# A hybrid recurrent and attention layer: heads innermost in q and k, keys stored twice, and a counted order of the recurrent projection's products

## The chip, the cores and the metric

One core of one Trainium2 chip runs the whole layer in one launch. The metric is the device time of an execution in microseconds (us). All sums below are made against one profiled execution and its trace.

## What is computed

The reference is one layer over 1024 latent tokens of width 1024 and 256 context tokens. Cut to what matters here:

```python
xn = modulate(rms_norm(x), sh1, sc1)                 # and cn for the context tokens
yg, xr, q, k, v, gr, gn = split_in(xn @ w_in + b_in) # each 1024 wide
xr = centred_dwconv(xr, conv_w, conv_b)              # 4 taps
# for both directions: r, i = sigmoid(xr @ wa), sigmoid(xr @ wi), 16 blocks of 64
a = exp(log_a); b = sqrt(-expm1(2 * log_a)) * (i * xr)
h = linear_recurrence(a, b, h0)                      # a scan over the tokens
y_rnn = (h_forward + h_backward) * gelu(yg)
q4, k4 = axial_rope(q), axial_rope(k)                # 16 heads of 64
y_na = neighbourhood_attention(q4, k4, v4, kc4, vc4, rpb)
mix = sigmoid(gr) * (y_rnn @ w_proj_rnn) + sigmoid(gn) * (y_na @ w_proj_na)
x = x + g1 * (mix @ w_out)
x = x + g2 * expert_choice_moe(modulate(rms_norm(x), sh2, sc2), ...)   # 16 experts
return rms_norm(x) * final_norm
```

## The kernel before, in words

Every product is made exact to about float32 by splitting each operand into a rounded high part and the rest: a product is three matmuls (`mm3`, lines 187 to 189): high by high, high by low, low by high. High parts are casts, low parts are subtractions. There is no scheduler: each engine runs its instructions in the order in which the program is written, and where two parts run beside each other, `weave` takes turns between two generators by a cost that each adds up in `done`.

The stages run one after the other.

1. **q, k, v** (about 60 to 389 us of the span). For each of four groups `g` of four heads, `rotary` makes 512 tokens at a time of q, then of k: TensorE (PE) fills PSUM tiles `pq`, ScalarE (ACT) evicts them to `qr`, VectorE (DVE) and GpSimd (POOL) rotate, and `out_parts` (lines 474 to 484) splits the result into `ohi` (ACT) and `olo` (DVE), three buffers each, and stores both to `d_q` or `d_k` in DRAM through SP's queue. A row of such a tile is one column of one head, and the four heads of the group are the outermost part of the row's number. v is evicted by DVE (`vo`, line 616) and stored by SP.
2. **The recurrent branch** (389 to 847 us), `stage_lru`. `proj` makes the eight blocks' inputs, gates and gelu branches; its products land in eight PSUM buffers `pp`. `chain` does, for each block `j`: the convolution `xc` (POOL, then DVE, lines 776 and 779), its high and low parts `xch` (ACT, line 783) and `xcl` (DVE), the gate matmuls, tanh evictions `tr`, `ti` (ACT), exponentials, and the scans (DVE). `tail(j)` adds both directions (POOL, line 736), multiplies by the gelu branch (DVE, line 744), splits the result into high (ACT, line 748) and low (POOL, line 749; DVE for the last block) and stores it to `d_yrh`, `d_yrl`. ACT also evicts the gates `tg` (line 729) and casts the streamed weights `w0h`, `w1h` (line 181).
3. **Attention and the recurrent projection** (847 to 1214 us), `stage_attn`. `attend` has 128 units `n` (pair of heads, strip of 128 queries, head of the pair). At step `n` it issues `score(n)` (four matmuls `sp`, then DVE's add of the bias and maximum, line 908), `turn(n-3)` (five transposes `pt` of 128 columns, copied out by ACT to `et`, line 933), `values(n-5)` (matmuls `pv`, for two units at every second step), `expo(n)` (ACT), and after the turn change `scale(n-1)` (DVE). Loads of the next heads (`load_head`, at steps 2 and 6 of 16), biases (4) and values (8) are written into the same steps, on SP's queue. `project` multiplies `w_proj_rnn` by y_rnn (from `d_yr`, tiles `x0h`, `x1h`, `x0l`, `x1l`, 1 MB each, fetched once for each half of the tokens): 128 products of three matmuls `pr`, 16 output blocks of 8 products each, two products to a turn of `weave`. Its weights come through the `Stream` S: 1 MB chunks in two raw buffers, each split as a whole by one ACT cast and one DVE subtraction of 128x2048 when a chunk is taken.
4. **Merge, router and experts** (1214 us to the end), not touched by the change.

SBUF is a stack at one end: attention's tiles take the place of the recurrent branch's, so a load into one waits until the old tile's last reader is done. Before, the first biases and v lie, among others, over `lwr0` (which serves as the last gate buffer) and `gel`.

The order inside attention is set by these lines:

```python
for n in range(N + 6):                 # attend: score(n), then
    if 0 <= n - 3 < N:
        turn(n - 3)
        done += 0.5
...
weave(attend(), project())
```

Of the kernel before, what the change touches and what calls it, by code (L numbers as in the profile page):

```python
# [55 lines left out]
IDLE = 1  # L56
A1, A2 = 3, 4
# [9 lines left out]
class Stream:  # L67
# [33 lines left out]
    def split(self, most=9, defer=False, pieces=1):  # L101
# [3 lines left out]
        while self.nsplit < min(self.nload, most) and self.chunks[self.nsplit][2] and self.pfree:  # L105
# [19 lines left out]
            self.nsplit += 1  # L125

# [47 lines left out]
class Kernel:  # L174
# [28 lines left out]
    def run(self):  # L203
# [16 lines left out]
        self.d_k = self.dram.tile([16, 128, NT], F32R, name="d_k")  # L220
# [95 lines left out]
    def stage_qkv(self):  # L316
# [337 lines left out]
    def stage_lru(self):  # L654
        nc, I, S = self.nc, self.I, self.S
        tgp, ctg = self.open_("tgp", side="right", bufs=1)
        p, cp = self.open_("lru2", side="right", bufs=1)
        last, clast = self.open_("lru3", side="right", bufs=1)
# [76 lines left out]
        def tail(j, M, done, step):  # L735
# [19 lines left out]
        def chain():  # L755
# [3 lines left out]
            for j in range(9):  # L759
# [23 lines left out]
                nc.scalar.copy(xch, xc)  # L783
# [55 lines left out]
        cfirst.__exit__(None, None, None)  # L839
        clast.__exit__(None, None, None)  # L840
        cp.__exit__(None, None, None)
# [5 lines left out]
    def stage_attn(self):  # L847
# [10 lines left out]
        def load_head(h):  # L858
# [101 lines left out]
        def attend():  # L960
            done = 0.0
# [6 lines left out]
            for n in range(N + 6):  # L968
                if n < N:
# [17 lines left out]
                    done += 0.55  # L987
                if 0 <= n - 3 < N:
                    turn(n - 3)
                    done += 0.5  # L990
                if 0 <= n - 5 < N:
                    values(n - 5)
                    done += 1.2 * (n % 2 == 0)
                if n < N:
                    expo(n)
                yield done
# [3 lines left out]
        def project():  # L1000
            done = 5.0
            yield done
            f = 1.75

# [17 lines left out]
            fetch_gate(0, 0)  # L1022
            for hf in range(2):
                cs = slice(hf * 512, (hf + 1) * 512)
                yh, yl = fetch(hf)
                done += 12.0
                yield done
                for i in range(4):
                    hi, lo = S.take8()
                    for x in range(2):  # L1030
# [5 lines left out]
                        for k in range(8):  # L1036
                            self.mm3(pm, hi[:, k, xs], lo[:, k, xs], yh[k // 4][:, k % 4], yl[k // 4][:, k % 4],
                                     k == 0, k == 7)
                            if k % 2 == 1:
                                done += 0.8 * f  # L1040
                                yield done
# [3 lines left out]
                        done += 2.0 * f  # L1045
                        yield done

        weave(attend(), project())
# [805 lines left out]
def _rope_tables():  # L1854
# [5 lines left out]
    ang = np.tile(ang, (4, 1)).astype(np.float64)  # L1860
# [3 lines left out]
def _qk_columns(base):  # L1864

    cols = []
    for g in range(4):
        for x in range(2):
            for h in range(4 * g, 4 * g + 4):
                for r in range(2):  # L1870
                    s = base + h * 64 + r * 32 + x * 16
                    cols.extend(range(s, s + 16))
# [109 lines left out]
```

## Time and profile before

| what | value |
|---|---|
| time, median of 3 runs | 2613.41 us (2612.39 to 2613.57) |
| profiled execution: time | 2614.25 us |
| profiled execution: span, first to last instruction | 2612.4 us |
| busy share of the span: PE, DVE, ACT, POOL | 95%, 72%, 59%, 12% |
| mean granted TensorE clock | 0.98 |
| DMA, mean over the span | 253 GB/s |

The span is 1.85 us shorter than the execution's own time, and that execution lies 0.8 us above the median of the three. Busy times of PE come from modelled ends of pipelined matmuls, so that a stretch that reads 95% busy still holds gaps; starts of matmuls are exact. Times in the rows are microseconds from the span's start. In a row of the timeline the bracket at the end is the engine's idle time just before it, and what ended that.

### The profile page before, as it was taken

The page shows a single profiled execution, that of the slowest core. Times are in us where ns is not written, and L with a number is a line of the kernel's source. Part 1 is how long each engine was busy: PE and PEld are TensorE (multiplying, and loading weights), DVE is VectorE, ACT ScalarE, POOL GpSimd, SP SyncE. Part 2 cuts the span into 40 slices and gives each one's busy share as a digit, 9 for nine tenths or more (in the row PEclk, how much of TensorE's full clock was granted, in tenths as well). Part 3 has the DMA queues.
Part 4 walks back from the last instruction along what each step waited for, and adds up shares of the span by engine and source line. Part 5 has one row for each costly group of instructions (what it writes and reads, how often), then busy time and mean ns, then how long its engine had stood idle before and what let it go on. Part 6 is the DMA issues. An engine that isn't in the chain of part 4 may idle for free.

```text
span 2612.4 us, 34543 instructions
## 1 busy us (share of the span) xinstructions
PE 2478.6 (95%) x13401; PEld 2038.4 (78%) x13401; DVE 1885.1 (72%) x2300; ACT 1534.0 (59%) x1699; POOL 302.4 (12%) x269
## 2 busy tenths in 40 slices
PE   7999999999999799999998699999999999999996
PEld 4887888777887687787987488888888888888885
DVE  5675643655565566666466888888888988898887
ACT  5321125556665456555343477777777777777776
POOL 1321110112120000000121000000000000000001
PEclk9999999999999899999999799999999999999998
DMA  8354531112215969655865799999999999999995
GB/s 276 135 205 165 186 131 47 67 71 87 74 70 166 302 209 281 197 160 181 265 234 185 285 358 369 369 370 381 375 376 384 374 379 369 370 370 369 370 370 202
DMA packets 145972, 661.82 MB, mean 253 GB/s; under 512 B 18000, under 2 KB 35552, under 8 KB 86928
## 3 DMA queue, kind: packets, MB, share of 16 engines
q1 hardware_dynamic: 122848, 585.18, 60.6%
q0 software_dynamic: 14864, 62.21, 7.1%
q10 hardware_dynamic: 8096, 12.21, 1.5%
q8 instruction: 106, 1.74, 0.3%
q14 instruction: 58, 0.48, 0.1%
HBM read 585.02 MB, written 74.53 MB: 252 GB/s over the span
## 4 chain that ended last, share of the span: by engine, by line
PE 76%; DVE 9%; ACT 7%; DMA 5%; issue 2%; ACTq 0%; SPq 0%; POOL 0%; POOLq 0%; DVEq 0%
PE pm L187 9%; PE pm L189 9%; PE pm L188 9%; PE po L187 5%; PE po L189 5%; PE po L188 5%; PE pv L948 2%; PE pp L187 2%; PE pp L188 2%; PE pp L189 2%; PE pt L931 2%; PE mm L187 2%; PE mm L189 2%; PE mm L188 2%; PE pq L187 2%
## 5 line engine op out<-in xcount | busy, mean ns | idle before, releaser
L98 DVE TENSOR_TENSOR w0l<-ring,w0h 128x2048 fp32r<-128x2048 f32 x110 | 251.9, 2290 | 76.7 <-ACT w0h L181 75.6
L98 DVE TENSOR_TENSOR w1l<-ring,w1h 128x2048 fp32r<-128x2048 f32 x110 | 251.8, 2289 | 58.8 <-ACT w1h L181 58.8
L181 ACT CAST w0h<-ring 128x2048 fp32r<-128x2048 f32 (+1 forms) x112 | 212.0, 1894 | 118.5 <-PE pm L189 49.9
L98 DVE TENSOR_TENSOR x0l<-ring,x0h 128x2048 fp32r<-128x2048 f32 x93 | 213.0, 2290 | 55.4 <-ACT x0h L181 55.4
L181 ACT CAST w1h<-ring 128x2048 fp32r<-128x2048 f32 x110 | 209.8, 1907 | 49.8 <-PE pv L189 23.6
L98 DVE TENSOR_TENSOR x1l<-ring,x1h 128x2048 fp32r<-128x2048 f32 x93 | 212.9, 2290 | 8.1 <-ACT x1h L181 7.0
L181 ACT CAST x1h<-ring 128x2048 fp32r<-128x2048 f32 x93 | 177.3, 1907 | 49.3 <-PE pm L189 31.6
L181 ACT CAST x0h<-ring 128x2048 fp32r<-128x2048 f32 x93 | 177.3, 1907 | 13.5 <-PE pm L189 13.5
L908 DVE CUSTOM_DVE_ANT_0 e<-sp,bias 128x640 f32<-128x640 f32 (+1 forms) x128 | 100.7, 787 | 80.9 <-PE sp L904 71.5
L1758 POOL DMA_INDIRECT d_acc<-y,idx x15 | 50.7, 3377 | 842.7 <-DVE y L1757 842.7
L933 ACT COPY et<-pt 128x640 f32<-128x640 f32 (+1 forms) x128 | 84.9, 663 | 105.0 <-PE pt L931 103.3
L916 ACT ACTIVATE e<-e,mx 128x640 f32<-128x640 f32 (+1 forms) x128 | 103.0, 805 | 42.7 <-DVE mx L910 41.5
L187 PE MATMUL pp<-xh,w1h 128*128 128x512 f32 (+1 forms) x304 | 116.3, 382 | 3.9 <-ACT tg L729 3.2
L188 PE MATMUL pp<-xl,w1h 128*128 128x512 f32 (+1 forms) x304 | 115.8, 381 | 0.0
L189 PE MATMUL pp<-xh,w1l 128*128 128x512 f32 (+1 forms) x304 | 115.7, 381 | 0.0
L187 PE MATMUL pp<-xh,w0h 128*128 128x512 f32 (+1 forms) x272 | 107.2, 394 | 4.6 <-ACT tg L729 3.5
L904 PE MATMUL sp<-k,q 128*128 128x256 f32 (+1 forms) x512 | 102.1, 323 | 8.1 <-DVE mx L908 6.5
L931 PE MATMUL pt<-ident,e 128*128 128x128 f32 x608 | 91.1, 279 | 18.7 <-ACT et L933 9.6
L188 PE MATMUL pp<-xl,w0h 128*128 128x512 f32 (+1 forms) x272 | 106.7, 392 | 0.0
L189 PE MATMUL pp<-xh,w0l 128*128 128x512 f32 (+1 forms) x272 | 106.6, 392 | 0.0
L187 PE MATMUL pm<-x1h,xeh 128*128 128x512 f32 x256 | 105.4, 412 | 0.0
L187 PE MATMUL pm<-w0h,xeh 128*128 128x512 f32 x256 | 102.7, 401 | 1.7 <-ACT xeh L1678 1.7
(472 smaller groups left out, 7173.3 us busy)
## 6 DMA issues: line engine op xcount, KB each, us to landing
ring<-w_exp_down SPq DMA_DIRECT2D x120, 1024.0 KB
ring<-w_exp_gate SPq DMA_DIRECT2D x117, 1024.0 KB
ring<-w_exp_up SPq DMA_DIRECT2D x117, 1024.0 KB
k<-d_k SPq DMA_DIRECT2D x64, 320.0 KB
wmr<-wm POOLq DMA_DIRECT2D x16, 1024.0 KB, 8.4
ring<-wrnn SPq DMA_DIRECT2D x16, 1024.0 KB
ring<-wqkv SPq DMA_DIRECT2D x12, 1024.0 KB
bias<-bias SPq DMA_DIRECT2D x16, 704.0 KB
```

The lines of the kernel that those rows point to most:

```text
L98: (engine or self.lo_engine).tensor_sub(lo, x, hi)
L181: self.nc.scalar.copy(hi, x)
L187: mm(out, wh, xh, start=first, stop=False)
L188: mm(out, wh, xl, start=False, stop=False)
L189: mm(out, wl, xh, start=False, stop=last)
L904: nc.tensor.matmul(sp[:, a:a + m], q[:, s * 128:(s + 1) * 128], ks[part][:, k0:k0 + m], start=part == 0, stop=part == 1)
L908: nc.vector.tensor_tensor_reduce(e[:, :w], sp[:, c0:c0 + w], b[:, b0:b0 + w], 1.0, -3.0e38, op0=ALU.add, op1=ALU.max, accum_out=mx[:, 0:1])
L916: nc.scalar.activation(e[:, :w], e[:, :w], AF.Exp, bias=mx[:, 1:2], accum_out=mx[:, 2:3])
L931: nc.tensor.transpose(pt[:, c * 128:(c + 1) * 128], e[:, c * 128:(c + 1) * 128], self.ident)
L933: nc.scalar.copy(et[:, :w], pt[:, :w])
L948: nc.tensor.matmul(pv[j * 64:(j + 1) * 64, (s % 4) * 128:(s % 4 + 1) * 128], v[:, t, j * 64:(j + 1) * 64], state[n - 1 + j][:, c * 128:(c ...
L1758: nc.gpsimd.indirect_dma_start(out=self.d_acc[:, :], out_offset=bass.IndirectOffsetOnAxis(ap=self.idx[:, e:e + 1], axis=0), in_=y[:, :], i ...
```

## The change

It has five parts.

1. **Columns of q and k with heads innermost.** `_qk_columns` and `_rope_tables` reorder weights and tables on the host, so that the number of a row in a tile is column times 4 plus head. The store in `out_parts` then has 32 columns outermost and 4 heads inside, where it had 4 heads outermost.
2. **Keys stored twice.** `d_k` becomes `[16, 2, 128, NT]`: each of high and low is stored to both halves of the partitions, and `load_head` fetches a part with one DMA of 128 partitions instead of two of 64. There are 48 more stores.
3. **The recurrent branch's copies.** `xch` and the high part in `tail` go from ACT to DVE, and the low part in `tail` from POOL to DVE for all blocks. The pools `lru2` and `lru3` change places in the stack, so that the first biases and v of attention lie over `tr` and `ti` and no longer over `lwr0` and `gel`.
4. **A counted order in attention.** `weave` is gone there. At step `n` the products of `project` that are due by then (64 spread over steps 11 to 61, 64 over 69 to 125) are issued one at a time, between `score(n)` and the transposes, and the transposes run four steps behind instead of three. y_rnn of the first half is fetched at step 0.
5. **Weights split in four pieces.** `split_by` splits a chunk in four casts and subtractions of 128x512, one every four products, where `take8` split it in one.

```diff
-            width = dst.shape[2]
-            for h, o in ((hi, 0), (lo, 64)):
-                nc.sync.dma_start(raw(dst.bitcast(F32), (g * 512 + o + part * 32) * width + tok,
-                                      [[128 * width, 4], [width, 32], [1, n]]), h[:, :n].bitcast(F32))
+            step, at = (128, ((0,), (64,))) if dst is self.d_q else (256, ((0, 64), (128, 192)))
+            for h, os in zip((hi, lo), at):
+                for o in os:
+                    nc.sync.dma_start(raw(dst.bitcast(F32), (g * 4 * step + o + part * 32) * width + tok,
+                                          [[width, 32], [step * width, 4], [1, n]]), h[:, :n].bitcast(F32))
...
-                for x in range(2):
-                    nc.sync.dma_start(t[x * 64:(x + 1) * 64].bitcast(F32),
-                                      self.d_k[h, part * 64:(part + 1) * 64].bitcast(F32))
+                nc.sync.dma_start(t.bitcast(F32), self.d_k[h, part].bitcast(F32))
...
-            eng, que = (nc.vector, nc.scalar) if j == 7 else (nc.gpsimd, nc.gpsimd)
-            nc.scalar.copy(hi, g)
-            eng.tensor_sub(lo, g, hi)
+            que = nc.scalar if j == 7 else nc.gpsimd
+            nc.vector.tensor_copy(hi, g)
+            nc.vector.tensor_sub(lo, g, hi)
...
-                nc.scalar.copy(xch, xc)
+                nc.vector.tensor_copy(xch, xc)
...
+        for c in range(0, 2048, 2048 // n):
+            cs = slice(c, c + 2048 // n)
+            self.k.hi_copy(hi[:, cs], x[:, cs])
+            self.lo_engine.tensor_sub(lo[:, cs], x[:, cs], hi[:, cs])
+            yield
...
-                if 0 <= n - 3 < N:
-                    turn(n - 3)
+                yield n
+                if 0 <= n - BEHIND < N:
+                    turn(n - BEHIND)
...
-                    hi, lo = S.take8()
+                    hi, lo = S.take8(most=0)
+                    more = S.split_by(4)
...
-        weave(attend(), project())
+        count, products = 0, project()
+        for n in attend():
+            if n == 0:
+                next(products)
+            due = min(64, (n - P0) * 64 // P1) + max(0, min(64, (n - P2) * 64 // P3))
+            while count < due:
+                next(products, None)
+                count += 1
+        for _ in products:
+            pass
```

Here `BEHIND` is 4 and `P0, P1, P2, P3` are 11, 50, 69, 56.

Three places show how instructions move. The first is ACT's queue in the recurrent branch, at the turn from block 1 to block 2, before:

```order
L820 ACTIVATE m<-m 128x1280 x2
L771 CAST lwh<-lwr_3416 128x512
L783 CAST xch<-xc 128x1280
L710 ACT_TABLE_LOAD
L710 ACTIVATE gel<-gel 128x1024
L181 CAST w1h<-ring_3947 128x2048
L729 ACTIVATE tg<-pp,par 128x512 x2
L748 CAST m<-gel 128x1024
L729 ACTIVATE tg<-pp,par 128x512
L802 ACTIVATE tr<-pp,par 128x512 x2
```

And the same place of the changed kernel (its line numbers are 20 to 25 higher):

```order
L844 ACTIVATE m<-m 128x1280 x2
L795 CAST lwh<-lwr_3464 128x512
L734 ACT_TABLE_LOAD
L734 ACTIVATE gel<-gel 128x1024
L202 CAST w1h<-ring_3995 128x2048
L753 ACTIVATE tg<-pp,par 128x512 x3
L826 ACTIVATE tr<-pp,par 128x512 x2
```

The casts `xch` and `m<-gel` are gone from this queue, and the three evictions `tg` stand together.

The second is SP's queue at the start of attention, from the first biases on, before:

```order
L881 DMA bias<-bias 128x1408 x2
L875 DMA v<-d_v 128x10x128
L863 DMA q<-d_q 128x1024
L868 DMA k_6452<-d_k 64x1280 x2
L868 DMA k_6455<-d_k 64x1280 x2
L881 DMA bias<-bias 128x1408 x2
L863 DMA q<-d_q 128x1024
L868 DMA k_6534<-d_k 64x1280 x2
L868 DMA k_6537<-d_k 64x1280 x2
L1020 DMA tgl<-d_tgr 128x512
L1011 DMA x0h<-d_yrh 128x4x512
L1011 DMA x1h<-d_yrh 128x4x512
```

And of the changed kernel:

```order
L904 DMA bias<-bias 128x1408 x2
L898 DMA v<-d_v 128x10x128
L1036 DMA tgl<-d_tgr 128x512
L1027 DMA x0h<-d_yrh 128x4x512
L1027 DMA x1h<-d_yrh 128x4x512
L1027 DMA x0l<-d_yrl 128x4x512
L1027 DMA x1l<-d_yrl 128x4x512
L93 DMA ring_6491<-wpr 128x2048
L1036 DMA tgl<-d_tgr 128x512
L887 DMA q<-d_q 128x1024
L891 DMA k_6511<-d_k 128x1280
L891 DMA k_6513<-d_k 128x1280
```

The four tiles of y_rnn and a chunk of weights now stand ahead of the loads of heads 2 and 3.

The third is PE's queue in the middle of the first half, for one unit before:

```order
L904 MATMUL sp<-k_6895,q 128x256
L904 MATMUL sp<-k_6898,q 128x256
L904 MATMUL sp<-k_6895,q 128x384
L904 MATMUL sp<-k_6898,q 128x384
L931 MATMUL pt<-ident,e 128x128 x5
L948 MATMUL pv<-et,v 64x128 x10
L187 MATMUL pr<-x1h,w0h 128x512
L188 MATMUL pr<-x1l,w0h 128x512
L189 MATMUL pr<-x1h,w0l 128x512
L187 MATMUL pr<-x1h,w0h 128x512
L188 MATMUL pr<-x1l,w0h 128x512
L189 MATMUL pr<-x1h,w0l 128x512
```

And of the changed kernel:

```order
L927 MATMUL sp<-k_7057,q 128x256
L927 MATMUL sp<-k_7059,q 128x256
L927 MATMUL sp<-k_7057,q 128x384
L927 MATMUL sp<-k_7059,q 128x384
L208 MATMUL pr<-x1h,w0h 128x512
L209 MATMUL pr<-x1l,w0h 128x512
L210 MATMUL pr<-x1h,w0l 128x512
L954 MATMUL pt<-ident,e 128x128 x5
```

The transposes no longer follow the scores directly: one product, sometimes two, stands between them, and no longer two together at the end of a unit.

## Rows read from the trace of the kernel before

**Rows 1.** Windows: us, PE PEld DVE ACT POOL busy, PEclk, DMA share, GB/s

```profile
847.00:1214.00 367.00, 332.01 (x2720) 275.96 (x2720) 231.30 (x679) 211.93 (x409) 24.83 (x46) 0.97 0.71 220
...
1480.00:2612.00 1132.00, 1111.63 (x5044) 894.34 (x5042) 1001.54 (x658) 853.76 (x683) 81.64 (x34) 0.99 0.94 362
```

**Rows 2.** Waits, 60 to 390 us: us in total, times, longest us

```profile
ACT ohi L478 <- DMA d_k<-ohi: 37.4, 8, 9.3
```

**Rows 3.** Timeline, 206 to 213 us, DVE and PE

```profile
206.58 0.43 DVE L480 TENSOR_TENSOR olo<-qr,ohi 128x256 fp32r<-128x256 f32 x1 [7.39 <-DMA d_k<-olo]
...
212.28 0.58 PE L187 MATMUL pv<-w1h,xh 128*128 128x256 f32 x1 [4.63 <-DVE vo L616]
```

**Rows 4.** Short stretches (windows): stores of k alone, after the stall, loads of k

```profile
360.00:366.00 6.00, 6.00 (x53) 6.00 (x53) 0.69 (x1) 0.62 (x2) 0.00 (x0) 1.00 0.26 102
...
212.00:218.00 6.00, 5.72 (x30) 5.72 (x31) 3.26 (x7) 0.00 (x0) 0.55 (x1) 0.58 0.97 308
...
826.00:836.00 10.00, 10.00 (x45) 8.05 (x44) 9.84 (x6) 3.12 (x3) 0.00 (x0) 1.00 1.02 275
```

**Rows 5.** Waits in the recurrent branch, 390 to 845 us

```profile
PE pp L187 <- ACT tg L729: 7.5, 3, 3.5
...
PE pp L188 <- DVE xcl L785: 3.1, 3, 1.9
```

**Rows 6.** Timeline of ACT behind the convolution of block 2

```profile
533.87 1.04 ACT L748 CAST m<-gel 128x1024 fp32r<-128x1024 f32 x1 [2.34 <-DVE gel L744]
...
534.82 0.68 ACT L729 ACTIVATE tg<-pp,par 128x512 f32<-128x512 f32 x1
```

**Rows 7.** The two stretches behind the PE stalls on tg (windows)

```profile
535.00:541.00 6.00, 5.45 (x25) 5.45 (x26) 0.06 (x1) 5.98 (x10) 3.62 (x6) 0.50 0.62 226
...
641.00:647.00 6.00, 5.89 (x14) 4.63 (x15) 1.49 (x1) 5.97 (x10) 3.17 (x6) 0.50 0.62 235
```

**Rows 8.** Forms of single lines: duration ns min/median/max, first and last start

```profile
L749 POOL TENSOR_TENSOR gel<-gel,m x7: 2362/2395/2416, 484.5 to 801.8; 128x1024 fp32r<-128x1024 f32 x7
L749 DVE TENSOR_TENSOR gel<-gel,m x1: 1224/1224/1224, 838.5 to 838.5; 128x1024 fp32r<-128x1024 f32 x1
...
L923 DVE TENSOR_SCALAR e<-e,mx x128: 486/553/557, 856.7 to 1208.7; 128x640 f32<-128x640 f32 x96, 128x512 f32<-128x512 f32 x32
...
L785 DVE TENSOR_TENSOR xcl<-xc,xch x8: 1491/1492/2666, 416.6 to 798.0; 128x1280 fp32r<-128x1280 f32 x8
```

**Rows 9.** Timeline at the start of attention: SP's biases, PE's stalls and unit 16

```profile
847.11 0.82 SPq L881 DMA_DIRECT2D bias<-bias  x2
...
853.25 1.44 PE L904 MATMUL sp<-k,q 128*128 128x256 f32 x4 [4.75 <-DVE mx L908]
...
889.06 0.79 PE L188 MATMUL pr<-x0l,w0h 128*128 128x512 f32 x1 [5.97 <-DMA x0l<-d_yrl]
...
899.76 0.64 PE L904 MATMUL sp<-k,q 128*128 128x256 f32 x4
```

**Rows 10.** Windows of eight units, tile pr alone: PE (instructions), PEld (instructions), DVE

```profile
899.70:919.30 19.60, 6.84 (x25) 4.21 (x24) 1.36 (x2) 1.00 0.93 266
919.30:945.50 26.20, 10.85 (x42) 7.51 (x42) 0.69 (x1) 1.00 0.46 158
...
1174.60:1190.10 15.50, 0.00 (x0) 0.00 (x0) 0.00 (x0) 1.00 0.22 73
...
899.70:1206.50 306.80, 96.29 (x361) 64.07 (x360) 10.96 (x16) 1.00 0.66 203
```

**Rows 11.** Timeline of two product matmuls that follow each other

```profile
906.66 0.40 PE L187 MATMUL pr<-x0h,w0h 128*128 128x512 f32 x1
906.90 0.39 PE L188 MATMUL pr<-x0l,w0h 128*128 128x512 f32 x1
```

**Rows 12.** ACT's cast of a whole chunk in attention, and PE's weight loads' waits, 900:1155

```profile
922.73 1.89 ACT L181 CAST w0h<-ring 128x2048 fp32r<-128x2048 f32 x1
...
PEld pt L931 <- ACT et L933: 15.8, 25, 1.1
```

More of the change, by code (lines that the diff above doesn't have):

```diff
@@ L56 @@
 IDLE = 1
+BEHIND = 4
+P0, P1, P2, P3 = 11, 50, 69, 56
 A1, A2 = 3, 4
@@ L125, in split, with split_by @@
             self.nsplit += 1
+    def split_by(self, n):
+        i = self.nsplit
+        if i >= self.nload or not self.chunks[i][2] or not self.pfree:
+            return
+        self.nsplit += 1
+        slot = self.pfree.popleft()
+        hi = slot[0].tile([128, 2048], F32R, name=slot[1] + "h", tag=slot[1] + "h")
+        lo = slot[0].tile([128, 2048], F32R, name=slot[1] + "l", tag=slot[1] + "l")
+        x, rslot = self.raws.pop(i)
+        for c in range(0, 2048, 2048 // n):
[3 more added lines that the diff above has]
+            yield
+        self.free.append(rslot)
+        self.parts[i] = (hi, lo, slot)
     def release(self):
@@ L219, in run @@
         self.d_q = self.dram.tile([16, 128, SEQ], F32R, name="d_q")
-        self.d_k = self.dram.tile([16, 128, NT], F32R, name="d_k")
+        self.d_k = self.dram.tile([16, 2, 128, NT], F32R, name="d_k")
         self.d_v = dr("d_v", [10, 128, D])
@@ L656, in stage_lru @@
         tgp, ctg = self.open_("tgp", side="right", bufs=1)
+        last, clast = self.open_("lru3", side="right", bufs=1)
         p, cp = self.open_("lru2", side="right", bufs=1)
-        last, clast = self.open_("lru3", side="right", bufs=1)
         first, cfirst = self.open_("lru1", side="right", bufs=1)
@@ L1022, in project @@
             fetch_gate(0, 0)
+            yh, yl = fetch(0)
             for hf in range(2):
                 cs = slice(hf * 512, (hf + 1) * 512)
-                yh, yl = fetch(hf)
-                done += 12.0
-                yield done
                 for i in range(4):
-                    hi, lo = S.take8()
+                    hi, lo = S.take8(most=0)
+                    more = S.split_by(4)
                     for x in range(2):
@@ L1036, in project @@
                         for k in range(8):
+                            yield
                             self.mm3(pm, hi[:, k, xs], lo[:, k, xs], yh[k // 4][:, k % 4], yl[k // 4][:, k % 4],
                                      k == 0, k == 7)
-                            if k % 2 == 1:
-                                done += 0.8 * f
-                                yield done
+                            if k % 4 == 2:
+                                next(more, None)
                         m = po.tile([128, 512], F32, name="m1", tag="m1", bufs=2)
@@ L1044, in project @@
                         nc.gpsimd.dma_start(self.d_m1[j, :, cs], m)
-                        done += 2.0 * f
-                        yield done
-        weave(attend(), project())
+                    for _ in more:
+                        pass
+                if hf == 0:
+                    yh, yl = fetch(1)
+                yield
+        count, products = 0, project()
[7 more added lines that the diff above has]
+        for _ in products:
+            pass
         cps.__exit__(None, None, None)
@@ L1859, in _rope_tables @@
     ang = np.concatenate([inv[:, None] * row[None, :], inv[:, None] * col[None, :]], 0).astype(np.float32)
-    ang = np.tile(ang, (4, 1)).astype(np.float64)
+    ang = np.repeat(ang, 4, axis=0).astype(np.float64)
     return np.cos(ang).astype(np.float32), np.sin(ang).astype(np.float32)
@@ L1868, in _qk_columns @@
         for x in range(2):
[L1869 to L1872, printed above, removed]
+            for r in range(2):
+                for i in range(16):
+                    cols.extend(base + h * 64 + r * 32 + x * 16 + i for h in range(4 * g, 4 * g + 4))
     return np.array(cols)
```

11 lines of the change are left out of this document (2 added, 9 removed).

## The prediction

> **What bounds the kernel now.** I read the stages first. In the experts, from 1480 us on, PE is busy for 1112 of 1132 us at nearly the full clock while DMA moves 362 GB/s [rows 1]: both are near their limits, the change touches nothing there, and so whatever is gained or lost before that stage is passed on to the end one for one. The stages that the change touches are ordered on PE: it is busy most of the time, and a loss shows as a gap ahead of a PE row, with a name behind it. So I went through those gaps stage by stage, and behind each gap looked at the granted clock, since a gap is often followed by a stretch at the lower of the two levels (1.2 instead of 2.4 GHz).
>
> In the first stage one gap matters: PE stands 4.63 us until `vo` is evicted, and DVE was late with that because it had stood 7.39 us for an `olo` buffer, which waits for a store to `d_k` [rows 3]. These stores are slow: where they run alone, DMA moves 102 GB/s at a share of 0.26 of the 16 engines [rows 4], as if four of them worked at full rate. ACT waits 37.4 us in all for the same stores [rows 2]. In the recurrent branch PE stands 7.5 us for gate evictions and 3.1 us for `xcl` [rows 5]. In attention two things are seen: the start, where unit 2 waits 4.75 us for the first unit's DVE step (its bias was issued only at 847.11 us) and the projection waits 5.97 us for y_rnn [rows 9]; and the pace, below.
>
> **Stores of q and k.** The bytes to `d_q` are the same, those to `d_k` double: 10.5 to 21 MB (32 stores of 256 KB and 16 of 128 KB, twice). If the stores still ran at 102 GB/s, this would add 103 us of store time. The trace of before has no store with 32 rows outermost; its nearest rows are bounded by that 102 GB/s below and by the loads of the same keys, 64 rows outermost, which fill all engines at 275 GB/s [rows 4]. I take 275, since the row's share of about 4/16 fits the four heads that stand outermost in the old store, and 32 no longer limits it. Then 29.4 MB of q and k need 107 us instead of 185, the buffers come free in time, and the gap goes. It is worth the 4.63 us, and behind it the stretch 212 to 218 us, where the clock was 0.58 and so 0.42 × 6 = 2.5 us were lost [rows 4]: together **7 us** (range 3 to 8; with stores at 102 GB/s a loss, below). The page "DMA: Bandwidth & Descriptors" of the Trainium skill (section "Why a DMA increments its semaphore by 16 and not by 1") says that a DMA runs on the largest number of engines, up to 16, that divides the slowest dimension of both sides, which makes 4 before and 16 now. The trace agrees with the 4; no row of before shows the 16. By that rule the term would be the same 7 us. The 48 further SP issues at about 0.5 us each lie beside PE's products; fetching a part of k by one DMA of 128 partitions instead of two saves issues on SP only, and I cost it at nothing.
>
> **Copies to DVE.** The nearest DVE row for a copy from one SBUF source is 0.55 us for 640 columns [rows 8]; twice that, 1.1 us, is an upper estimate for 1280; ACT takes 1.04 us for 1024 [rows 6]. The subtraction of 1024 columns costs DVE 1.22 us where POOL took 2.39 [rows 8]. DVE so gets about 1.1 + 0.9 + 1.2 = 3.2 us for each block, which lies where it waits for ACT's `ti`. ACT loses two casts, and what counts more, two waits: it runs in order, and evictions `tg` stood behind a cast that waited for DVE. In block 2 the third `tg` came at 534.82 because `m<-gel` had stood 2.34 us and took 1.04 [rows 6]; without it that eviction follows the two before it at about 531.5, 3.3 us earlier. ACT still waits behind the convolution for the gelu branch, so the gap shrinks and does not vanish everywhere. Of the 7.5 us on `tg` I take 6.5 off, of the 3.1 us on `xcl` 1.5. The two stretches of 6 us behind the `tg` gaps, both at clock 0.50 [rows 7], lost 3 us each; I take 5 of these 6. Sum **13 us** (range 4 to 16).
>
> One thing speaks against it. `xcl` took 2.67 us once, where its median is 1.49 [rows 8]; POOL's addition of both directions ran at that time, and PE waited for that `xcl`. New copies on DVE can meet the same addition; this is a rival below. "SBUF — State Buffer" of the Trainium skill (section "Who interferes with whom") says that a DVE copy in a two-port mode and a GpSimd instruction shut each other out for a whole instruction. The trace agrees in that one case of eight; by that rule a copy could cost up to a whole POOL addition, and a term of 13 us could fall below 0.
>
> **The start of attention.** Before, the first score starts after the last `tg`, its bias is issued at 847.11, and unit 16, the first of heads 2 and 3, starts at 899.76 with 24 of the 384 product matmuls done (360 follow) [rows 9, 10]. Now the first biases and v wait for the scans' tiles; the scans lie ahead of DVE's last step of block 7 at 838.5 [rows 8], so these tiles are free at least 8 us before 847.11. Unit 0 starts at about 846 with its bias there. Units without products take 15.5 / 8 = 1.94 us [rows 10]: unit 12 at 869.3. Four units more at 1.81 (below) and 6 products of 3 × 0.233 us (0.24 and 0.23 us from start to start [rows 11]) make 880.7, 19 us earlier. Two products fewer are done by then (1.4 us). The y_rnn tiles (4 MB) now go ahead of heads 2 and 3: from the first y tile to the end of head 3 there are 4.2 + 1.3 + 1.8 + 1.4 + 1.8 = 10.5 MB, which take 34 to 38 us at 275 to 308 GB/s [rows 4], from about 847, so 881 to 885 against a need at 883. I allow 2.6 us for it: **15 us** (range 3 to 18). The second slow stretch, behind the wait for y_rnn, is in this sum.
>
> **The pace.** From unit 16 to the last score there are 306.7 us, 112 units and 360 product matmuls [rows 10]. At 0.233 us the products take 83.8, so a unit takes 223 / 112 = 1.99 us. In the first eight of these units it was (19.6 - 24 × 0.233) / 8 = 1.75, in the next eight (26.2 - 42 × 0.233) / 8 = 2.05. What differs is a whole cast of 1.89 us on ACT between the copies `et`, and PE's weight loads wait for `et` 15.8 us [rows 12]. Now a piece takes a quarter of that, and a unit's transposes have a step more and a product ahead of them, so nothing that they need is fresh. I take 1.80 for the 101 units that have products among them (1.75, and 0.05 for the more frequent change between kinds of matmul), and 1.95 for the 11 without: 203 instead of 223, **19 us** (range 0, the old pace, to 26, all at 1.75). The pipeline is a step longer at the end, and one product is left over: **-2 us**.
>
> **Sum.** 7 + 13 + 15 + 19 - 2 = 52 us off the span of 2612.4, so 2560.4; the execution lay 1.85 us above its span and 0.8 above the median, which gives 2614.25 - 52 - 0.8 = 2561.4, and I say **2561**. About 0.2% (5 us) is what a measurement of this kernel can tell from no change.
>
> **Rivals.** *The recurrent chain takes over* (chance 0.07): with PE's gaps gone PE waits for DVE's chain instead. For it: the 3.1 us on `xcl`, just in time in three blocks. Against: the waits taken from ACT shorten the chain itself. The 13 us fall to 4: 2570. *POOL and DVE hold each other up* (0.04): each of seven additions meets a copy or `xcl`, at 1.2 us each [rows 8], 8 us on the chain. Against: it happened once in eight. The 13 us fall to 5: 2569. *The pace stays* (0.10): ACT's and DVE's lengths, not the lump, set 1.99 us, and one product ahead of the transposes changes nothing; for it, units without any cast still take 1.94. 2580. *Heads 2 and 3 come late* (0.08): with 250 GB/s the 10.5 MB end at 889, and unit 17 waits for them, and the clock falls behind that wait; the 15 us fall to 3: 2573. *Stores stay at 102 GB/s* (0.05): then a group's k needs 51 us of stores where its products took 28 us of PE time (120 matmuls of 512 columns at 0.233 us); three buffers cover a few us, so some 20 us in each of four groups, 80 in all, stand against 45 gained elsewhere: 2648, slower. It decides below about 200 GB/s, where twice the bytes take as long as before. *It cancels* (0.02): some loss of this size for the gains, within 0.2%.
>
> My forecast has 0.64. Single failures end at 2570 to 2580, two of them together near 2592; all upper bounds together (8 + 16 + 18 + 26 - 2 = 66) give 2547. The range 2545 to 2592 leaves out the slow stores, no change, and a little of the rest. Faster 0.93, same 0.02, slower 0.05.
>
> **What would show it.** Right: stretches with only stores to `d_k` at far more than 102 GB/s, and no wait of ACT for `d_k`; no PE gap on `tg` over 1 us and no stretch at clock 0.5 behind it; biases issued before the last gate matmul, unit 16 near 36 us after unit 0 instead of 52; eight units with products at 1.8 us each after taking off the products. Wrong: PE rows that wait for `xcl` in most blocks, for k or bias of heads 2 and 3 around unit 16, for `et` as often as before, or for the `pr` buffer's eviction between two blocks of products, which I cost at nothing because a unit's other matmuls mostly stand between them (if they don't, 16 times about 0.8 us, 13 us).

## The result, and the profile after

The changed kernel takes **2555.36 us** (median of four, 2554.85 to 2557.05) against 2613.49 for the kernel before: a ratio of 0.978 (95% interval 0.9763 to 0.9797). Its profiled execution has a span of 2554.0 us, 58.4 less than before; forecast were 52 less and 2561.

Where the 58.4 us lie is read from the starts of PE's rows: the first `pp` (end of the first stage), the first `sp` (unit 0), the first `sp` of units 16 and 127, and the first `mm` of the merge. The differences, in us:

| stretch | before | after | gain | forecast |
|---|---|---|---|---|
| first stage, to the first `pp` | 388.8 | 381.7 | 7.1 | 7 |
| recurrent branch, to unit 0 | 458.5 | 447.1 | 11.4 | 13 |
| start of attention, units 0 to 16 | 52.5 | 30.7 | 21.8 | 15 |
| pace, units 16 to 127 | 305.9 | 287.9 | 18.0 | 19 |
| end, unit 127 to the merge | 9.6 | 12.0 | -2.4 | -2 |
| merge, router, experts | 1397.1 | 1394.7 | 2.4 | 0 |

The last row is not of the change: over all the kernels below it took 1394.6 to 1397.1 us, whatever was changed ahead of it.

*First stage and start of attention.* Three windows of the changed kernel; columns as in [rows 1]:

```profile
355.00:360.00 5.00, 5.00 (x45) 5.00 (x44) 3.38 (x3) 0.84 (x1) 0.00 (x0) 1.00 0.86 304
836.00:846.00 10.00, 9.22 (x83) 7.51 (x84) 8.51 (x29) 7.94 (x16) 0.00 (x0) 1.00 1.04 399
846.00:856.00 10.00, 10.00 (x93) 8.58 (x93) 7.17 (x23) 7.18 (x16) 1.09 (x2) 1.00 1.02 414
```

The first lies among the stores of k: 304 GB/s at a share of 0.86, where before it was 102 at 0.26 [rows 4]. The other two answer to the loads of [rows 4], 275 GB/s: the queues' share is as full as it was, but it moves 399 to 414. Nothing in the share told of that room. The waits of 60 to 382 us (us in total, times, longest), against 37.4 in [rows 2], and those of PE in the recurrent branch, 382 to 828 us, against [rows 5]:

```profile
ACT ohi L499 <- DMA d_k<-ohi: 13.5, 4, 8.6
DVE olo L501 <- DMA d_k<-olo: 5.7, 4, 2.7
PE pp L208 <- DVE vo L640: 0.9, 1, 0.9
```

```profile
PE pp L209 <- DVE xcl L809: 3.6, 3, 2.3
PE pp L208 <- DVE xch L807: 1.2, 1, 1.2
...
PE pp L208 <- ACT tg L753: 0.4, 1, 0.4
```

The stall on `vo` (4.63 us in [rows 3]) and those on `tg` (7.5 us) are gone; `xcl` stays. ACT still waits 13.5 us for stores to `d_k`, where the prediction's sign of being right was none; PE's wait for `vo` at the end of the stage, 0.9 us, is as before. SP's queue at the start of attention, and PE's first row of unit 16, answer to [rows 9]:

```profile
819.76 0.86 SPq L904 DMA_DIRECT2D bias<-bias  x2
...
828.34 0.43 SPq L1027 DMA_DIRECT2D x0h<-d_yrh  x1
...
835.80 0.57 SPq L887 DMA_DIRECT2D q<-d_q  x1
```

```profile
859.45 0.72 PE L927 MATMUL sp<-k,q 128*128 128x256 f32 x4
```

The biases go out 9.0 us ahead of unit 0 (828.76), and y_rnn's first tile now goes out at unit 0, not 21 us behind it; PE waits for no load from there to unit 16, and the clock is at its full level.

*Pace.* Waits of PE and PEld between units 16 and 127, first before (899.76 to 1206 us), then after (859.45 to 1147.31):

```profile
PEld pt L931 <- ACT et L933: 21.3, 35, 1.1
PE pt L931 <- DVE e L923: 8.1, 9, 1.8
PE pt L931 <- ACT et L933: 7.1, 24, 0.4
```

```profile
PEld pt L954 <- ACT et L956: 3.2, 6, 0.6
...
PE pt L954 <- ACT et L956: 1.5, 5, 0.4
...
PE pr L208 <- DVE m L1058: 1.1, 1, 1.1
```

From the last score matmul of a unit to the first transpose it was 0.366 us in the mean (111 times; 384 columns at the full clock are 0.16, estimated from 512 in 0.233 [rows 11], scaled). The loss was not spread evenly. Where a unit's scores stood behind values it was 0.165 us (27 units), behind products 0.245 (48 units), and 0.68 in the 36 units whose scores stood directly behind the transposes of the unit ahead, with nothing else between the two sets of transposes. Two units of before, far from any product or cast:

```profile
1173.62 0.74 PE L904 MATMUL sp<-k,q 128*128 128x256 f32 x4
1174.19 0.71 PE L931 MATMUL pt<-ident,e 128*128 128x128 f32 x5
1174.65 0.72 PE L904 MATMUL sp<-k,q 128*128 128x256 f32 x4
1175.74 0.77 PE L931 MATMUL pt<-ident,e 128*128 128x128 f32 x5 [0.36 <-ACT et L933]
```

After, the scores are followed by a product in 101 of 111 cases, 0.180 us on, and by transposes in 10, still at 0.41; from a product to the transposes it is 0.236, no wait. So what was lost there was 111 x (0.366 - 0.16) = 23 us, and is now 101 x (0.02 + 0.003) + 10 x 0.25 = 5 us. These 18 us are the bulk of the gain, though not the same sum. Counted by rows, each from its start to the start of the next, the pace gains 13.9 us at the scores (18 less 4.5, since no unit's scores now follow a product, and behind values or transposes the second score matmul starts later), 2.6 at the products, although there are two products more, and 1.6 at the transposes.

### The profile page after: what moved, and what is told of

Read it like the earlier page. It is cut to its first block, busy times and chain, and to the rows that moved or that the text cites. A ratio compares the mean times of both kernels' runs of the same rounds, so it can differ in the third digit from the quotient of the medians.

```text
span 2554.0 us, 34491 instructions
## 1 busy us (share of the span) xinstructions
PE 2459.5 (96%) x13401; PEld 2026.6 (79%) x13401; DVE 1908.8 (75%) x2347; ACT 1518.8 (59%) x1707; POOL 281.9 (11%) x262
## 3 DMA queue, kind: packets, MB, share of 16 engines
q8 instruction: 105, 1.72, 0.3%
## 4 chain that ended last, share of the span: by engine, by line
PE 85%; DVE 6%; ACT 4%; DMA 2%; issue 1%; ACTq 0%; POOL 0%; POOLq 0%; SPq 0%; DVEq 0%
PE pm L208 9%; PE pm L209 9%; PE pm L210 9%; PE po L208 5%; PE po L210 5%; PE po L209 5%; PE pp L209 3%; PE pp L210 3%; PE pp L208 3%; PE pv L971 3%; PE sp L927 3%; PE pt L954 3%; PE pq L208 2%; PE pq L210 2%; PE pq L209 2%; PE mm L208 2%
## 5 line engine op out<-in xcount | busy, mean ns | idle before, releaser
L101 DVE TENSOR_TENSOR w0l<-ring,w0h 128x2048 fp32r<-128x2048 f32 x106 | 242.7, 2290 | 59.5 <-ACT w0h L202 58.2
L202 ACT CAST w0h<-ring 128x2048 fp32r<-128x2048 f32 (+2 forms) x124 | 214.2, 1728 | 118.9 <-PE pm L210 50.5
L101 DVE TENSOR_TENSOR w1l<-ring,w1h 128x2048 fp32r<-128x2048 f32 x106 | 242.6, 2289 | 45.7 <-ACT w1h L202 45.7
L202 ACT CAST w1h<-ring 128x2048 fp32r<-128x2048 f32 (+1 forms) x122 | 211.9, 1737 | 48.4 <-PE pm L210 22.6
L202 ACT CAST x0h<-ring 128x2048 fp32r<-128x2048 f32 x93 | 177.3, 1907 | 13.5 <-PE pm L210 13.5
L210 PE MATMUL pm<-w0h,xel 128*128 128x512 f32 x256 | 102.0, 399 | 0.0
```

What stands on the lines that cost most here:

```text
L101: (engine or self.lo_engine).tensor_sub(lo, x, hi)
L202: self.nc.scalar.copy(hi, x)
L210: mm(out, wl, xh, start=False, stop=last)
```

## The experiments

All times are medians; "before" was 2608 to 2613 us beside them. The stretches of each profiled execution, in us, named as above:

| kernel | time | first stage | recurrent | start | pace | end |
|---|---|---|---|---|---|---|
| before | 2613.49 | 388.8 | 458.5 | 52.5 | 305.9 | 9.6 |
| changed | 2555.36 | 381.7 | 447.1 | 30.7 | 287.9 | 12.0 |
| e1, heads outermost | 2657.36 | 481.7 | 445.2 | 30.7 | 287.8 | 12.0 |
| e2, stores and load alone | 2591.74 | 381.5 | 457.2 | 40.3 | 306.0 | 9.6 |
| e3, copies alone | 2595.40 | 389.9 | 445.6 | 47.4 | 305.6 | 9.6 |
| e4, pools not swapped | 2558.32 | 382.4 | 445.4 | 33.1 | 288.1 | 12.0 |
| e5, order and pieces alone | 2587.20 | 385.0 | 458.2 | 37.3 | 297.1 | 12.0 |
| e6, whole casts | 2557.04 | 380.5 | 446.8 | 30.7 | 288.8 | 12.0 |
| e7, three behind | 2553.47 | 381.8 | 443.9 | 30.8 | 287.7 | 10.3 |
| e8, keys stored once | 2564.63 | 382.5 | 443.9 | 30.7 | 297.3 | 12.0 |
| e10, one load | 2599.07 | 387.0 | 458.5 | 40.4 | 307.2 | 9.6 |
| e11, stored once, one load | 2555.13 | 382.5 | 445.6 | 30.7 | 287.9 | 12.0 |
| e12, products to the end | 2558.80 | 382.1 | 445.5 | 30.7 | 287.8 | 14.9 |
| e13, tail's copies alone | 2600.54 | 386.4 | 447.9 | 52.1 | 305.7 | 9.6 |

Read down a column: the first stage is 385.0 to 389.9 with the old stores and 380.5 to 382.5 with the new, so one pair of traces can be off by 2 us; the start and the pace repeat to some tenths.

**e1, heads outermost, keys still stored twice.** Columns and tables as before, and in the store:

```diff
-                                          [[width, 32], [step * width, 4], [1, n]]), h[:, :n].bitcast(F32))
+                                          [[step * width, 4], [width, 32], [1, n]]), h[:, :n].bitcast(F32))
```

> The changed kernel with the old columns (four heads outermost in the tiles and in the stores' patterns), keys still stored twice; the same bytes go to the same places. If what stands outermost in the pattern sets the rate of a store, the stores to d_q and d_k run near 102 GB/s again, 29.4 MB need 288 us of a stage of 320 us, bursts of k (51 us of stores against 28 us of products) fill the three buffers in each group, ACT and DVE wait for d_k far more than the 37.4 and 36.8 us of the kernel before, and the time is 2575 to 2635 us. If the pattern does not matter, and only the chance order of the stores made the stall, the time stays within 3 us of 2555.

Measured: 2657.36 us, ratio to before 1.0179 (1.0162 to 1.0196). Waits of the first stage in its trace, and a window of stores alone:

```profile
DVE olo L501 <- DMA d_k<-olo: 100.7, 11, 13.1
ACT ohi L499 <- DMA d_k<-ohi: 89.2, 10, 12.4
...
PE pv L208 <- DVE vo L640: 61.5, 4, 28.0
```

```profile
440.00:470.00 30.00, 16.02 (x119) 15.62 (x117) 5.45 (x7) 2.61 (x3) 0.00 (x0) 0.77 0.27 102
```

The same bytes, in another order of dimensions, move at 102 GB/s, and the first stage takes 100 us more than in the changed kernel. It was worse than expected because PE stands for `vo`, which DVE evicts in order behind an `olo` that waits for a store: the same chain as in [rows 3], four times. So the pattern decides, and storing k twice without the new columns would have made the kernel slower.

**e2, the first two parts alone.** The kernel before with the diff's first two pieces and the host's columns.

> The kernel before with the first two parts alone (heads innermost, keys stored twice). By the term of the prediction the stall of 4.63 us and the low clock behind it go: 7 us less, 2606.5 us, with the first matmul of the recurrent branch near 381.7 us instead of 388.8. Rival: the recurrent branch takes the gain back, since its chain starts with the same data a little later than PE: 2611 to 2614 us.

Measured: 2591.74 us, ratio 0.993 (0.9913 to 0.9946). The first stage ends at 381.5, as expected, and the recurrent branch gives nothing back. But 12.2 us more are gained where nothing was expected, in attention's start. This led to e10.

**e10, the load alone.** The kernel before, with a part of k fetched at once. The source pattern has the 64 rows outermost and inside them a dimension of 2 with step 0, so that each row is read twice running; the rows of q are stored with high and low alternating, to match.

```diff
-                for x in range(2):
-                    nc.sync.dma_start(t[x * 64:(x + 1) * 64].bitcast(F32),
-                                      self.d_k[h, part * 64:(part + 1) * 64].bitcast(F32))
+                nc.sync.dma_start(t.bitcast(F32), raw(self.d_k.bitcast(F32), (h * 128 + part * 64) * NT,
+                                                      [[NT, 64], [0, 2], [1, NT]]))
```

> The kernel before with one thing changed: a part of k is fetched by one DMA of 128 partitions that reads the same 64 rows twice, instead of by two DMAs of 64 partitions (q's high and low rows alternate in DRAM, so that they meet the right key rows). In the second run the start of attention was 12.2 us shorter though only the stores and this load had changed; DMA moved about 280 GB/s there in the kernel before and about 400 GB/s in that run at the same full share. If the width of the load is the cause, the start takes about 40 us instead of 52.5 and the time is 2599 us (2597 to 2602). Rival: the start gained from the other phase in which it began: 2609 to 2612 us. Second rival: a read with a repeated outer dimension is itself slow, the loads fall behind and PE waits for k: above 2615 us.

Measured: 2599.07 us, ratio 0.9948 (0.9932 to 0.9965), the start 40.4 us: the first theory, to the microsecond. Of the 12.1 us, 10.9 lie in units 8 to 16, where PE had waited for y_rnn. A window of the same piece of the start, before and then in this kernel:

```profile
860.00:870.00 10.00, 9.58 (x81) 8.04 (x80) 7.97 (x26) 8.04 (x17) 0.00 (x0) 0.89 1.02 300
```

```profile
855.00:865.00 10.00, 9.19 (x66) 7.30 (x64) 9.21 (x31) 8.18 (x18) 0.00 (x0) 0.89 1.02 415
```

At the same share of 1.02, 415 GB/s against 300. These windows hold other loads too, but the trace's DMA records single out k: the transfer of one of its rows (5120 bytes, 4096 of them in attention) took 351 ns in the mean before and 334 in e8, both by halves, and 207 here and 203 in the changed kernel. The Trainium skill states the rule in "SBUF — State Buffer", section "Can I just issue two DMAs to hit both halves?": only one transfer that spans all 128 partitions reaches all of the ports, and two for the halves take turns. The traces agree that halves are slower, with the numbers above; that two of them take turns no run here shows by itself.

**e8, keys stored once, loaded in halves.** The changed kernel with `d_k`, its store offsets and `load_head` as before, columns kept.

> The changed kernel with heads innermost, but keys stored once and fetched by two DMAs of 64 partitions for each part, as before. If the width of the load matters only where DMA is short, the first stage stays at 381 to 382 us, the pace stays, and attention's start (30.7 us in the changed kernel) grows by 4 to 12 us: 2559 to 2567 us. Rival: in the new order no product is due before step 11, so that the slower loads are hidden: 2554 to 2557 us.

Measured: 2564.63 us. The size was right, the place was not: the start stays at 30.7, and the loss of 9.3 us stands behind unit 16. PE's rows there:

```profile
865.82 0.55 PE L929 MATMUL sp<-k,q 128*128 128x256 f32 x1 [5.57 <-DMA k<-d_k]
868.02 0.98 PE L929 MATMUL sp<-k,q 128*128 128x256 f32 x3 [1.65 <-DMA k<-d_k]
```

This is the forecast's rival "heads 2 and 3 come late", at unit 17 as named. It does happen in this order, with loads by halves; the wide loads are what prevents it. PE has the last of k for unit 17 at 868.02 us, 41.6 us behind unit 0.

**e11, keys stored once, one load that reads them twice.** The changed kernel with the load of e10, and with 48 stores fewer.

> The changed kernel with keys stored once (10.5 MB less to write, 48 stores fewer) and a part of k fetched by one DMA of 128 partitions that reads 64 rows twice. If the second store costs nothing beside the products of q and k, the time is that of the changed kernel, 2553 to 2557 us. If the second store still costs DMA time that something waits for, 2550 to 2553 us. Rival: the repeated read is slower than a plain one, and the start of attention grows: 2560 us or more.

Measured: 2555.13 us, every stretch as in the changed kernel. Of the part "keys stored twice" only the shape of the load is worth anything; the second store costs nothing and brings nothing.

**e5, the last two parts alone.** The kernel before with `attend`, `project`, the loop and `split_by` of the changed kernel.

> The kernel before with the last two parts alone: the counted order with y_rnn early, transposes four steps behind, and weights split in four pieces. By either theory the 111 units from unit 16 to the last take about 288 us instead of 306, and the end 2 us more. If the start of attention gained from this order, it takes 31 to 35 us instead of 52.5: 2576 to 2580 us. If it gained from the wider loads of k, it stays at 40 us or more, with heads 2 and 3 late behind y_rnn: 2584 to 2596 us.

Measured: 2587.20 us, ratio 0.9905 (0.9889 to 0.9922). The total is that of the second theory, but its reason is only half right: the start is 37.3 us, so the order alone gains 15.2 there, and the pace loses 9.2 of its 18 at unit 17, as in e8 (PE waits for `k<-d_k` there). What the start lacks against the changed kernel, 6.6 us, lies in the first eight units (18.32 us against 11.71): the first biases go out 0.2 us ahead of unit 0 instead of 9.0, and DVE's step of unit 0 begins 5.2 us behind it instead of 0.85. So the 21.8 us of the start are the order (15.2) and the early biases (6.6). The wide loads, worth 12.1 us in the start of the kernel before, add nothing to it in the new order (e8 has 30.7 us too); there they save the 9.3 us at unit 17.

**e4, pools in their old places.** The changed kernel with `lru2` and `lru3` opened and closed as before.

> The changed kernel with lru2 and lru3 in their old places. If the early bias is what made attention's start 21.8 us shorter rather than the predicted 15, the first biases come about 20 us later, unit 2 waits some 5 us again and the clock falls behind it: 2562 to 2568 us. Rival: the start is shorter because no products stand among the first twelve units and y_rnn is there in time, whatever the bias does: within 2 us of 2555.

Measured: 2558.32 us (2555.58 to 2558.89), the start 33.1 instead of 30.7 us; the biases go out at 825.23, 2.6 us ahead of unit 0. Neither number was met: the places of the pools are worth 2.4 us in the start, not the 7 or more that the first theory wanted. That is not all that early biases bring. In their old places the pools still let the biases go ahead of unit 0, since the copies alone bring them there (2.8 us ahead in e3); e5, which has neither the copies nor the new places, takes 18.3 us for the first eight units, e4 14.2, the changed kernel 11.7.

**e3, the copies alone; e13, only those of the tail.** The kernel before with

```diff
-                nc.scalar.copy(xch, xc)
+                nc.vector.tensor_copy(xch, xc)
```

and the tail's three lines of the diff; e13 has the tail's alone.

> The kernel before with xch and both parts of the tail's split on DVE, pools in their old places. If the 11.4 us that the recurrent branch lost in the changed kernel come from the copies, the time is 2602 us (2600 to 2604), with no wait of PE for tg over 1 us. Rival: part of the 11.4 us came from elsewhere (the pools' places, or the branch starting in another phase of the weights' stream): 2606 to 2610 us.

> The kernel before with only the tail's split moved (high part from ACT, low part from POOL, both to DVE); xch stays on ACT. The copies together made the recurrent branch 12.9 us shorter. By the prediction's reading of ACT's queue the cast m<-gel held back the evictions tg: most of it comes from the tail, 448 to 451 us for the branch instead of 458.5, 2601 to 2604 us in all. Rival: xch, which waits on ACT for the convolution and starts the gates, is the larger half: 453 to 458 us, 2606 to 2611 us.

Measured: e3 2595.40 us, ratio 0.9942 (0.9925 to 0.9958); e13 2600.54, 0.9963 (0.9949 to 0.9977). The recurrent branch takes 445.6 and 447.9 us instead of 458.5. So 10.6 of 12.9 us come from the tail, as the prediction read it from ACT's queue in [rows 6]. In e3 the start gains 5.0 us besides, which the expectation had not seen: the first biases go out 2.8 us ahead of unit 0 and the first eight units take 13.8 us instead of 19.0. With the tail's copies alone (e13) they go out 0.6 us ahead, and the start gains 0.4.

**e6, whole casts; e7, three steps behind.** The changed kernel with one of

```diff
-                    more = S.split_by(4)
+                    more = S.split_by(1)
```

```diff
-BEHIND = 4
+BEHIND = 3
```

> The changed kernel with each weight chunk split by one cast and one subtraction of 128x2048 (at the third product of a chunk) instead of four of 128x512. If the lump of 1.89 us between the copies et is what made a unit 1.99 us, the 111 units from unit 16 to the last take 294 to 300 us instead of 288, and the time is 2561 to 2567 us. Rival: the fourth step behind and the product ahead of the transposes cover the lump: 287 to 289 us, 2554 to 2557 us.

> The changed kernel with the transposes three steps behind the scores, as before, and the rest of the order kept. If the fourth step is needed so that nothing that the transposes want is fresh, the 111 units take 292 us or more instead of 288, and the time is 2557 us or more, the shorter end of 2 us included. Rival: a product ahead of the transposes is cover enough: the units stay at 288 us, the end is 2 us shorter, 2552 to 2554 us.

Measured: e6 2557.04 us, pace 288.8; e7 2553.47 (2551.17 to 2555.48), pace 287.7 and the end 1.7 us shorter. Both rivals hold: neither the four pieces nor, with them kept, the fourth step is needed for the pace. In both kernels, as in the changed one, the ten units that have no product between scores and transposes still take 0.41 us there, and the 101 others 0.18. e7 was the fastest of all, but its interval (0.9773 to 0.9806 of before) overlaps that of the changed kernel, so only the 1.7 us at the end are shown, by the traces.

**e12, products to the end.**

```diff
-P0, P1, P2, P3 = 11, 50, 69, 56
+P0, P1, P2, P3 = 11, 50, 69, 62
```

> The changed kernel with the second 64 products spread over 62 steps instead of 56, so that they reach steps 125 to 131, where PE now stands about 3 us in four gaps while the last units' transposes wait for et. If these gaps can take products and the earlier units do not slow down, the time is 2552 to 2554 us. Rival: units with fewer products among them lose as much as the end gains (1.94 us for a unit without products against 1.72 to 1.85 with them): 2555 to 2557 us.

Measured: 2558.80 us, worse than either expectation. Six more products stand behind unit 127 and fill its gaps, and the end is 2.9 us longer; but the units ahead, with these 18 matmuls fewer (18 x 0.233 = 4.2 us), took as long as before. PE waits there for the eviction of `pr`, 4.8 us in five waits instead of 1.1. One of them, from the timeline of all engines:

```profile
1140.42 0.69 DVE L979 TENSOR_TENSOR yol<-pv,yoh 128x512 fp32r<-128x512 f32 x1 [0.90 <-ACT yoh L977]
...
1140.83 0.40 PE L210 MATMUL pr<-x1h,w1l 128*128 128x512 f32 x1
...
1141.68 0.82 DVE L931 CUSTOM_DVE_ANT_0 e<-sp,bias 128x640 f32<-128x640 f32 x1
...
1142.65 0.69 DVE L1058 SCALAR_TENSOR_TENSOR m<-tgl,pr 128x512 f32<-128x512 f32 x1
...
1143.39 0.50 PE L208 MATMUL pr<-x0h,w1h 128*128 128x512 f32 x1 [1.15 <-DVE m L1058]
```

The block's last product ends at about 1141.2; its eviction stands on DVE behind a unit's score step, and that is late because DVE had first to make `yol`, the low part of attention's own result, which comes once in eight units. This is the wait that the prediction had named and costed at nothing, and which steps the block ends fall on decides it. With 62 steps a block takes 7.75 of them, and all seven block ends between products in the second half fall next to a `yol`: four wait 1.1 us, and three, with values behind them on PE, 0.05 to 0.3. With 56 steps a block takes 7, and one end falls there, the one that waits 1.1 us. Six other block ends of the changed kernel have only transposes and scores behind them too, but no `yol` ahead: their eviction starts 0.6 to 0.7 us behind the start of the block's last matmul instead of 1.8, and PE does not wait.

## Why the prediction was right, step by step

**Stores, 7 us: right.** 7.1 measured, 5.5 as the mean of the eight kernels with the new stores (381.9) against the five with the old (387.4). The mechanism is shown by e1: the outer dimension of the pattern. The rival at 102 GB/s, 2648 us, was a fair price for a case that did not come: e1 gave 2657. The rate itself was taken too low (275; the stores moved 304), which cost nothing here. The rule cited from the Trainium skill ("DMA: Bandwidth & Descriptors", section "Why a DMA increments its semaphore by 16 and not by 1") says that the engines used are the largest number up to 16 that divides the slowest dimension of both sides: 4 in e1, 16 in the changed kernel. The traces agree, with 102 GB/s for 4 outermost and 304 for 32.

**Copies, 13 us: right.** 11.4 in the pair of traces, 12.7 between the means of four kernels with the old copies (458.1) and nine with the new (445.4). DVE paid less than estimated for each block: rows of `xch` 0.83, of the tail's copy 0.69 and of its low part 1.23, 2.75 us instead of 3.2. The 1.5 us expected from `xcl` did not come (3.6 us instead of 3.1), and a wait of 1.2 us for `xch` is new. In all PE's waits in this stage fell from 11.6 to 5.1 us, and what it lost at the low clock, worked out from the granted clock, from 8.5 to 3.4 us: the forecast's 5 for the clock was right. The prediction misread one row: POOL's addition and DVE do not meet once in eight blocks. In both kernels, at each of the seven additions on POOL, the DVE instruction with two inputs that starts behind it ends only when the addition is over: `xcl` twice (2.67 and 2.66 us before, 3.54 and 3.57 after, 1.49 alone), and five times the first piece of `xc` (2.6 us for 256 columns that take 0.48 alone). The rival was so at work before the change already, and hardly grew; the first `xcl` cost 2.3 us of PE. Nor is the case that the prediction took for the cited rule on copies one of a copy: `xcl` is a subtraction with two inputs. The new copy `xch`, with one input, took 0.83 us all eight times, also the two times that it started 0.2 us ahead of an addition.

**Start, 15 us: mechanism right, size off, and one step of it failed.** The step that failed is "fetching a part of k by one DMA of 128 partitions instead of two saves issues on SP only, and I cost it at nothing". It is worth 12.1 us alone (e10), and 9.3 us in the changed kernel (e8): without it the rival "heads 2 and 3 come late" would have come, since the forecast had them there 35 to 39 us behind unit 0 and e8 shows 41.6. The cause of the error is the reading of 275 GB/s at a share of 1.02 [rows 4] as full engines: the share counts the time that packets are under way, and these were slow (351 ns for a row of k, where the wide loads took 203). The same number made the allowance of 2.6 us for heads 2 and 3, which was not needed at 399 to 414 GB/s.

The size is compared best on the stretch itself, because the forecast's 15 us also hold 1.3 us for a unit 0 at 846 and take off 1.4 us for two products that move to the pace. From unit 0 to unit 16 the forecast was 883.3 - 846 = 37.3 us, and it took 30.7. Of these 6.6 us, 2.6 are the allowance, 0.7 a product fewer than the six that were costed, and 3.3 the units: the first four, which have no transposes behind them yet, took 4.1 us in all instead of 4 x 1.94 = 7.8, while units 8 to 16 took 0.5 us more than costed.

**Pace, 19 us: right in size, wrong in two of its three causes.** Without the products at 0.233 us, a unit took 1.83 us in the mean instead of 2.00; forecast were 1.81 and 1.99 (223 less 203 is 20, of which the sum took 19). Of the eleven groups of eight units with nine or more products ten took 1.72 to 1.85 us a unit, and one, which holds the wait of 1.1 us for `pr`, 2.00; those with fewer products took 1.92 to 2.05. But "what differs is a whole cast of 1.89 us" falls with e6 (0.9 us for all casts) and with the rows of before, which have seven whole casts in this stretch against 36 units with the long gap, and "a step more" falls with e7. What is left of the sentence is the product ahead of the transposes, and the trace shows the gain in that place (23 us down to 5): between two sets of transposes PE now has a product to do, where in 36 units it had only scores. Two things stay open. With whole casts and three behind at once it was not run. And no run tells the place of the product from its even spread: before, 48 units had their products ahead of the scores and lost only 0.08 us each, so one product to every unit, wherever it stands in it, may do as well.

**End, -2 us: right** (-2.4; e7 shows 1.7 of it as the price of the fourth step). **`pr` at nothing: right here** (1.1 us), and by luck: e12 pays 4.8. The reason given, that a unit's other matmuls stand between, is not what decides: it is whether the block ends next to a `yol`.

## What to carry to other kernels

Before costing a load or a store, look at its shape on both sides: here a load over 128 partitions at once instead of two over 64, and a store with 32 rows outermost in DRAM instead of 4, were worth 10 us and more, while half the bytes of k to store (e11) were worth nothing. Compare GB/s, since a full share of the DMA engines can hide a third of their rate. When two sets of transposes follow each other closely and another engine has to copy the first out, see that independent matmuls stand between them, one lot to each unit, before cutting that engine's work in pieces. And when an order is tuned by numbers, look at what the evicting engine has in front of it where each block ends: six steps more at one end cost more than they gave.

## What the runs showed of the hardware that was not expected

- Two DMAs of 64 partitions each for a tile, against one of 128: 264 to 300 GB/s against 382 to 415 (windows of 10 us at attention's start; before and e8, then changed and e10), at shares of 1.02 to 1.05 in both; 334 to 351 ns for a row of 5120 bytes against 203 to 207.
- A load that reads each of 64 rows twice, by a dimension of 2 with step 0 inside the rows' own dimension, is not slow: e10 and e11 moved 415 and 413 GB/s with it, 207 and 209 ns a row. A repeated dimension outermost of all was not tried.
- POOL and DVE: a DVE instruction with two sources in SBUF that started during POOL's addition ended only behind it, seven times of seven in either kernel; the copy `xch`, with one source, twice started 0.2 us ahead of an addition and took its usual 0.83 us. In the changed kernel `xcl` took 3.54 us instead of 1.49 beside it, and ended 1.34 us after it:

```profile
468.87 3.54 DVE L809 TENSOR_TENSOR xcl<-xc,xch 128x1280 fp32r<-128x1280 f32 x1
```

```profile
468.22 2.85 POOL L760 TENSOR_TENSOR m<-m 128x1024 f32<-128x1024 f32 x1
```
